# Weight sums of a fast matrix product, formed by DMA in DRAM: begun two stages earlier, each in a tensor of its own

## The chip, the cores and the metric

One core of one Trainium2 chip runs the kernel. The metric is the device time of one execution in microseconds (us). The engines that matter are TensorE (PE, matrix products), VectorE (DVE), ScalarE (ACT), GpSimd (POOL) and SyncE (SP, which issues most DMA transfers here). All of them run their own instruction lists in order and meet through semaphores.

## The reference

One encoder layer on 512 positions of width 2048, in float32:

```python
h = rms_norm(x) * (1.0 + scale[:, None]) + shift[:, None]
aq, ak, av, ag, gq, gk, gv, gg, lr_f, lr_b = jnp.split(h @ w_in[layer], PROJ_SPLITS, axis=-1)
# 16 heads of attention over three dilated windows, merged by their denominators
a_out = att.reshape(B, S, ATT_WIDTH) * jax.nn.silu(ag)
# 4 heads of gated linear attention (GLA), scanned in both directions
g_out = g_o * jax.nn.silu(gg)
y = jnp.concatenate([a_out, g_out], axis=-1) @ w_out[layer]
return rms_norm(x + gate[:, None] * y) * final_gain
```

`scale`, `shift` and `gate` come from a product of `silu(c)` with a 2048 x 6144 matrix.

## The kernel before

Every large product is made from float32 numbers split in two parts, hi and lo; three PE products (hi hi, hi lo, lo hi) take the place of one. A weight tile of 512 KB is loaded by SP (`fetch`) into one of four `raw` buffers, ACT makes its hi part, DVE its lo part (`split_hi`, `split_lo`).

The stages follow each other on PE, whose order is written by hand:

1. Stages `a` and `b`: 16 steps of k each, with the sums that give `scale` and `shift` beside them. A planner (`_plan`) with due times orders the other engines here.
2. Units `qk2`, `qk4`, `qk6`, `gk`: eight groups of weights each, with the attention of two pairs of heads mixed in. The keys' halves (`ks`, `kl`) are moved by small DMAs from POOL's queue.
3. The v stage (GLA's values) as a fast matrix product: seven block products `a b f c d e f g` in place of eight, 28 steps of 512 KB weights. Some weight operands are sums of quadrants of the weight matrix: T1 = B11+B12, T2 = T1+B22, T3 = T2+B21, U = B12+B22. Some left operands are sums of quadrants of h, kept in DRAM and loaded as 256 KB halves (`hrb` to `hre`, by `h_load`).
4. Gated units `ag0`, `ag1`, `gg0`, `gg1`, with the four GLA heads and the sums for `vbias` and `gate` (`sumv`, `sumg`: loads of 512 KB or 1 MB that DVE multiplies and adds up) mixed in.
5. The output stage: two fast matrix products (pair 0 and pair 1), with the same sums T1, T2, T3, U of `w_out`'s quadrants; at last the final norm and the stores.

The weight sums cost PE nothing: DMAs on POOL's queue form them in DRAM. `sum_begun` (L333) copies one 512 KB quarter of the first operand into the sum's tensor, `sum_ended` (L336) adds the second operand to it (an accumulating DMA). `weight_sums` issues them from the list `sum_dmas`, so many per weight group as `SUM_DMAS` says; a small POOL instruction on the group's hi part (`seen`, L351) holds them back until that group has been split. `sum_in_place` adds T2 onto T1's tensor, and T3 onto T2's, where no copy is made; it can start only when the last load of the old sum has landed, so these additions run inside the v stage (T2 beside product `b`, T3 beside `c`) and inside the output stage (T3 beside `c` of either pair).

On SP the loads stand in one list. In the v stage step z asks for the weights of step z+3 first and then for h's halves up to step z+3. The framework's scheduler orders ACT, DVE, POOL and SP outside stages `a` and `b` by priority and by when data is ready, except where `keep_in_program_order` pins them.

In the GLA scan (`states`, L874 to L900) DVE writes a state into half 0 of the tile `pair`, POOL multiplies it by the decay into half 1 (L892), and DVE adds the next product to that into half 0 again (L894); ACT scales each state for PE (L899).

Of the kernel before, what the change touches and what calls it, by code (L numbers as in the profile page):

```python
# [10 lines left out]
F32 = mybir.dt.float32  # L11
# [3 lines left out]
ALU = mybir.AluOpType  # L15
# [6 lines left out]
KT = D // P  # L22
# [111 lines left out]
def block_kernel(ctx: ExitStack, tc: tile.TileContext, a: dict):  # L134
# [200 lines left out]
    def sum_ended(pair, name, q):  # L335
        return nc.gpsimd.dma_start(dsum[pair, name, q], quadrant(pair, SUMS[name][1], q), accum_op=ALU.add,  # L336
                                   max_dma_last_dim=4096)
# [431 lines left out]
    def sum_of(kind, m):  # L769
# [15 lines left out]
        def part(z, c, to, first):  # L785
# [22 lines left out]

    def some_sums(name, how="halves", lead=1.0, begin=0.0):
        r = next_sums(SUMS_IN.get(name, len(sum_work)), how)  # L810
        if begin:
            r = [(load, lambda go=go: tc.keep_in_program_order(go())) for load, go in r]
        n = len(r) / (1 - begin)
        loads = [(max(begin + (q + 0.7 - lead) / n, 0.1 / n), x[0]) for q, x in enumerate(r)]
        return sorted(loads + [(begin + (q + 0.7) / n, x[1]) for q, x in enumerate(r)], key=lambda x: x[0])

    def gla_head(h):
# [57 lines left out]
        def states(d):  # L875
            def go():
# [7 lines left out]
                for j, c in enumerate(x["order"]):  # L884
                    o = 256 * (j % 2)
                    kv = pkv[j // 2][:, o:o + 256]
                    st = pair[:, 0, :]
                    if prev is None:
                        nc.vector.tensor_scalar(st, kv, sc[:, 2, c:c + 1], None, op0=ALU.mult)  # L889
                    else:  # L890
                        dc = pair[:, 1, :]
                        nc.gpsimd.tensor_scalar(dc, prev, sc[:, 1, c:c + 1], 1.0,  # L892
                                                op0=ALU.mult, op1=ALU.mult)
                        stt(st, kv, sc[:, 2, c:c + 1], dc, op0=ALU.mult, op1=ALU.add)  # L894
# [70 lines left out]
    def unit(name, natural, side=(), lr=None):  # L965
# [5 lines left out]
        for g in range(KT // 2):  # L971
# [505 lines left out]
    for pair, n, q in steps:  # L1477
# [152 lines left out]
```

## Time and profile before

| | |
|---|---|
| median of 3 runs | 937.34 us (937.13 to 938.41) |
| the profiled execution's own time | 938.63 us |
| its span, first to last instruction | 936.9 us |
| TensorE busy | 911.5 us, 97% of the span |
| VectorE, ScalarE, GpSimd busy | 718.1, 482.9, 144.1 us |
| DMA queue q1 (SP) | 182.11 MB, 53.8% of 16 engines' span |
| DMA queue q0 (POOL) | 51.52 MB, 23.2% of 16 engines' span |
| granted TensorE clock, mean | 0.993 |

In a row of a view by stretches stand, for each engine, its busy us and in brackets its instructions, then the granted clock, the DMA engines' mean busy share and the GB/s moved. In a row of a timeline stand start, duration, engine, line and operation; the bracket at its end says how long the engine had waited and for whom. SPq is SP's queue of DMA issues.

### The profile page before, as it was taken

How to read it: one execution, taken by the hardware profiler on the slowest of the kernel's cores; microseconds unless marked ns; L12 is line 12 of the kernel's file. 1: busy time of each engine (PE TensorE's matmuls, PEld its weight loads, DVE VectorE, ACT ScalarE, POOL GpSimd, SP SyncE). 2: the span in 40 equal slices, each digit the busy share in tenths (PEclk: the TensorE clock that was granted, in tenths of full speed). 3: DMA queues.
4: the chain of work that ended last, by engine and by line, in shares of the span. 5: the costliest groups of instructions: out<-in, count | busy, mean ns of one | idle time of the engine just before them, and what ended most of it. 6: DMA issues, size and time to landing. Idle time of an engine off the chain costs nothing.

```text
span 936.9 us, 11887 instructions
## 1 busy us (share of the span) xinstructions
PE 911.5 (97%) x4225; PEld 748.9 (80%) x4225; DVE 718.1 (77%) x1071; ACT 482.9 (52%) x771; POOL 144.1 (15%) x221
## 2 busy tenths in 40 slices
PE   9999999999999999999989999979999999999995
PEld 7888888888888888888767888868888888788785
DVE  7998899688878788898726986657696769577386
ACT  4543533564655555555525744534464448445355
POOL 7400000051332321221110022111111000000100
PEclk9999999999999999999999999999999999999998
DMA  9999796498996886896999785676554458967954
GB/s 338 412 411 416 266 314 237 136 316 226 251 328 237 223 241 183 222 252 182 326 258 300 258 291 196 221 201 202 160 180 142 172 181 296 316 216 235 308 200 180
DMA packets 60044, 234.95 MB, mean 251 GB/s; under 512 B 7784, under 2 KB 8336, under 8 KB 53584
## 3 DMA queue, kind: packets, MB, share of 16 engines
q1 hardware_dynamic: 48176, 182.11, 53.8%
q0 software_dynamic: 11376, 51.52, 23.2%
q8 instruction: 33, 0.54, 0.2%
q10 hardware_dynamic: 432, 0.55, 0.2%
q14 instruction: 27, 0.22, 0.1%
HBM read 220.44 MB, written 51.46 MB: 290 GB/s over the span
## 4 chain that ended last, share of the span: by engine, by line
PE 74%; DMA 13%; DVE 7%; issue 2%; ACT 2%; SPq 0%; DVEq 0%; ACTq 0%
PE op L1469 6%; DMA sumg<-in_wg 6%; PE ps_qk L168 5%; PE ps_qk L169 5%; PE ps_qk L170 5%; PE stb L170 3%; PE stb L168 3%; PE stb L169 3%; PE o L728 3%; PE sta L169 3%; PE vp L1149 3%; PE sta L170 3%; PE sta L168 3%; PE t L715 3%; PE oq L1469 3%; PE ps_gg L168 3%
## 5 line engine op out<-in xcount | busy, mean ns | idle before, releaser
L269 DVE CUSTOM_DVE_ANT_0 cb<-cb,sb,c_bcond 128x2048 f32<-128x2048 f32 (+1 forms) x32 | 74.0, 2313 | 6.0 <-DMA cb<-in_wm 5.9
L702 ACT ACTIVATE p<-p,st 128x512 f32<-128x512 f32 x64 | 46.0, 719 | 24.2 <-DVE st L699 22.3
L699 DVE CUSTOM_DVE_ANT_0 p<-s,g 128x512 f32<-128x512 f32 x64 | 43.4, 682 | 1.7 <-PE s L696 1.5
L336 POOL DMA_DIRECT2D T<-in_w_o x24 | 17.7, 736 | 165.3 <-DMA raw_o0c<-T 93.3
L269 DVE CUSTOM_DVE_ANT_0 sumg<-sumg,sb,c_bcond 128x1024 f32<-128x1024 f32 (+1 forms) x16 | 23.7, 1483 | 19.4 <-DMA sumg<-in_wg 19.4
L715 PEld LDWEIGHTS t<-c_ident,p 128*128 128x128 f32 x256 | 31.8, 141 | 8.4
L715 PE MATMUL t<-c_ident,p 128*128 128x128 f32 x256 | 38.3, 272 | 0.0
L704 DVE TENSOR_SCALAR p<-p,st 128x512 f32<-128x512 f32 x64 | 31.0, 485 | 1.7
L269 DVE CUSTOM_DVE_ANT_0 sumg<-sumg,sb,gate 128x1024 f32<-128x1024 f32 x13 | 16.7, 1282 | 17.3 <-DMA sumg<-in_wg 17.3
L899 ACT ACTIVATE sq<-pair,sc 128x256 f32<-128x256 f32 x24 | 12.2, 507 | 27.9 <-DVE pair L889 16.9
L695 PE MATMUL s<-ks,qs 128*128 128x512 f32 x64 | 25.3, 395 | 0.0
L696 PE MATMUL s<-kl,qs 128*128 128x512 f32 x64 | 25.0, 391 | 0.0
L1024 POOL DMA_DIRECT2D gqd<-gqt x1 | 0.6, 586 | 151.3 <-ACT gqt L537 151.3
L703 DVE RECIPROCAL st<-st 128x1 f32<-128x1 f32 x64 | 10.2, 159 | 12.6 <-ACT p L702 12.5
L291 POOL TENSOR_SCALAR lnm<-lnm,rel 16x207 f32<-16x207 f32 (+7 forms) x14 | 18.9, 1363 | 5.0 <-DMA lnm<-in_lnm 5.0
L473 ACT ACTIVATE h_hi<-xt,shift 128x512 fp32r<-128x512 f32 x16 | 11.4, 719 | 11.3 <-DVE shift L269 11.3
L731 ACT ACTIVATE pair<-o 64x512 f32<-64x512 f32 x16 | 9.5, 595 | 14.9 <-PE o L728 14.8
L336 POOL DMA_DIRECT2D T1v<-in_w_gv x12 | 9.4, 783 | 47.4 <-DMA raw_ovb<-T1v 28.9
L930 PE MATMUL go<-qi,sq 128*128 128x128 f32 x96 | 15.9, 275 | 0.0
L892 POOL TENSOR_SCALAR pair<-pair,sc 128x256 f32<-128x256 f32 x16 | 8.6, 537 | 47.2 <-DVE pair L889 41.2
L269 DVE CUSTOM_DVE_ANT_0 sumv<-sumv,shb 128x1024 f32<-128x1024 f32 (+1 forms) x8 | 11.9, 1488 | 5.0 <-DMA sumv<-in_wv 5.0
L932 ACT ACTIVATE gsq<-go 128x512 f32<-128x512 f32 x8 | 4.8, 597 | 21.1 <-PE go L930 21.1
(1841 smaller groups left out, 3244.3 us busy)
## 6 DMA issues: line engine op xcount, KB each, us to landing
cb<-in_wm SPq DMA_DIRECT2D x31, 1024.0 KB, 11.3
T<-in_w_o POOLq DMA_DIRECT2D x32, 512.0 KB, 7.9
sumg<-in_wg SPq DMA_DIRECT2D x26, 512.0 KB, 4.2
raw_qk<-in_w_qk SPq DMA_DIRECT2D x24, 512.0 KB, 5.3
rawb<-in_w_sb SPq DMA_DIRECT2D x16, 512.0 KB, 6.4
T1v<-in_w_gv POOLq DMA_DIRECT2D x16, 512.0 KB, 9.7
U<-in_w_o POOLq DMA_DIRECT2D x16, 512.0 KB, 8.1
raw_ag<-in_w_ag SPq DMA_DIRECT2D x16, 512.0 KB, 4.5
```

The costliest lines, as they stand in the source:

```text
L168: mm(ps, lh, rh, start=first, stop=False)
L169: mm(ps, ll, rh, start=False, stop=False)
L170: mm(ps, lh, rl, start=False, stop=last)
L269: return nc.vector.tensor_tensor_reduce(out=w, in0=w, in1=with_, op0=ALU.mult, op1=ALU.add, scale=1.0, scalar=init, accum_out=dst)
L336: return nc.gpsimd.dma_start(dsum[pair, name, q], quadrant(pair, SUMS[name][1], q), accum_op=ALU.add, max_dma_last_dim=4096)
L699: nc.vector.tensor_tensor_reduce(out=t, in0=ps, in1=gt[h][:, P * i:P * i + 512], op0=ALU.add, op1=ALU.min, scale=1.0, scalar=3e38, accum_o ...
L702: act(t, t, AF.Exp, bias=st[:, 0:1], scale=-1.0, accum_out=st[:, 1:2])
L704: nc.vector.tensor_scalar(t, t, st[:, 2:3], None, op0=ALU.mult)
L715: nc.tensor.transpose(pk[:, kt * P:kt * P + P], t[:, kt * P:kt * P + P], ident)
L728: mm(po, vv[h // 4][:, kt, h % 4, :], parts[w][:, kt, :], start=kt == 0 and w == 0, stop=kt == 3 and w == 1)
L1149: mm(ps, l_, r_, start=first and x == 0, stop=last and x == 2, skip_group_check=not new)
L1469: mm(ps[:, c], l_, r_[:, c], start=first and z == 0, stop=last and z == 2, skip_group_check=not new)
```

## The change

Four things.

- `sum_in_place` is gone. T2 and T3 are begun by a copy like the others and ended by an addition, so 96 transfers in place of 80: 48 additions as before, 48 copies in place of 32.
- The list starts earlier and ends later: eight copies in the second half of stage `b` (planner tasks `wsum`), 48 transfers in `qk2` to `gk` as before, four copies in the v stage, nine transfers in each gated unit (before: eight in `ag0`, eight in `ag1`, none behind them).
- In the v stage h's halves are asked for ahead of the weights. The sums `sumv` that run beside it are laid out by other positions (`sums_in_parts`).
- The GLA states alternate between the two halves of `pair`; the decayed state goes into the tile that ACT later fills with the scaled state (`sq2`).

```diff
-    def sum_in_place(pair, name, q):
-
-        dsum[pair, name, q] = dsum[pair, SUMS[name][0], q]
-        sum_ended(pair, name, q)
-
-    sum_dmas = [(f, pair, name, q) for pairs, names in ((("v",), ("T1", "U")), ((0, 1), ("T1", "U")), ((0, 1), ("T2",)))
+    sum_dmas = [(f, pair, name, q) for pairs, names in ((("v",), ("T1", "U")), (("v",), ("T2",)), (("v",), ("T3",)), ((0,), ("T1", "U")), ((0,), ("T2",)),
+                                     ((1,), ("T1", "U")), ((0,), ("T3",)), ((1,), ("T2",)), ((1,), ("T3",)))
                 for f in (sum_begun, sum_ended) for name in names for pair in pairs for q in range(4)]
...
-    SUM_DMAS = {"qk2": 2, "qk4": 2, "qk6": 1, "gk": 1, "ag0": 1, "ag1": 1, "gg0": 1}
+    SUM_DMAS = {"qk2": 2, "qk4": 2, "qk6": 1, "gk": 1, "ag0": 1.125, "ag1": 1.125, "gg0": 1.125, "gg1": 1.125}
...
+    for k in range(8, KT):
+        task(("wsum", k), "POOL", 1.5, [("wh", "b", k)] + ([("wsum", k - 1)] if k > 8 else ["rows"]), 50,
+             lambda k=k: weight_sums(spl["b", k][0], 1, lambda x: x))
...
-                    parts=[(load(2, c, b8_), part(0, c0, half, init)), (lambda: None, part(1, c1, dst, half))])
+                    parts=[(load(2, c, b8_), part(0, c0, half, init), part(1, c1, dst, half))])
...
+    def sums_in_parts(name):
+        r = next_sums(SUMS_IN[name], "parts")
+        return [((s_ // 3 + (0.02, 0.5, 0.64)[s_ % 3]) / len(r), x) for s_, x in enumerate(y for z in r for y in z)]
...
-                    st = pair[:, 0, :]
+                    st = pair[:, j % 2, :]
+                    if j % 2 == 0:
+                        sq2 = T2(f"sq{n}{j}")
...
-                        dc = pair[:, 1, :]
+                        dc = sq2[:, o:o + 256]
...
+        for y in range(z, z + 4):
+            h_load(y)
         for ahead in (2, 3):
             fetch(i + ahead)
-        if n in "bc":
-            sum_in_place("v", "T2" if n == "b" else "T3", q)
-        for y in range(z, z + 4):
-            h_load(y)
+        if z in (0, 2, 23, 25):
+            weight_sums(wts[i][0], 1)
...
-        if n == "c":
-            sum_in_place(pair, "T3", q)
```

The rows below are the instruction lists of the two kernels. In POOL's rows at the v stage, names that end in v and a digit are sums for the v stage, T202 is quarter 2 of T2 for output pair 0, `16x8192` is a copy and `128x1024` an addition. Before:

```order
L351 TENSOR_SCALAR seen_131<-gk7h_3914 1x1
L336 DMA U12_2733<-in_w_o3 128x1024
L351 TENSOR_SCALAR seen_131<-ova0h_4001 1x1
L336 DMA U13_2735<-in_w_o3 128x1024
L336 DMA T1v0_1548<-in_w_gv1 128x1024
L336 DMA T1v1_1550<-in_w_gv1 128x1024
L336 DMA T1v2_1584<-in_w_gv1 128x1024
L336 DMA T1v3_1586<-in_w_gv1 128x1024
L336 DMA T1v0_1548<-in_w_gv0 128x1024
L336 DMA T1v1_1550<-in_w_gv0 128x1024
L336 DMA T1v2_1584<-in_w_gv0 128x1024
L336 DMA T1v3_1586<-in_w_gv0 128x1024
```

And the same place now:

```order
L347 TENSOR_SCALAR seen_131<-gk7h_3934 1x1
L336 DMA T202_3602<-in_w_o1 128x1024
L347 TENSOR_SCALAR seen_131<-ova0h_4021 1x1
L336 DMA T203_3682<-in_w_o1 128x1024
L347 TENSOR_SCALAR seen_131<-ova0h_4021 1x1
L333 DMA T110_4095<-in_w_o2 16x8192
L347 TENSOR_SCALAR seen_131<-ova2h_4103 1x1
L333 DMA T111_4149<-in_w_o2 16x8192
L347 TENSOR_SCALAR seen_131<-ovf3h_4688 1x1
L333 DMA T112_4746<-in_w_o2 16x8192
L347 TENSOR_SCALAR seen_131<-ovg1h_4754 1x1
L333 DMA T113_4787<-in_w_o2 16x8192
```

The eight additions in place are gone; two copies stand at the stage's first steps (groups ova0, ova2) and two near its end (ovf3, ovg1).

POOL's rows at the start of unit `gg0`. Before:

```order
L351 TENSOR_SCALAR seen_131<-gg00h_5687 1x1
L336 DMA T213_5237<-in_w_o3 128x1024
L351 TENSOR_SCALAR seen_131<-gg01h_5751 1x1
L351 TENSOR_SCALAR seen_131<-gg02h_5814 1x1
L351 TENSOR_SCALAR seen_131<-gg03h_5884 1x1
```

And now:

```order
L347 TENSOR_SCALAR seen_131<-gg00h_5712 1x1
L336 DMA T300_5530<-in_w_o0 128x1024
L336 DMA T301_5566<-in_w_o0 128x1024
L347 TENSOR_SCALAR seen_131<-gg01h_5777 1x1
L336 DMA T302_5602<-in_w_o0 128x1024
L347 TENSOR_SCALAR seen_131<-gg02h_5841 1x1
L336 DMA T303_5665<-in_w_o0 128x1024
L347 TENSOR_SCALAR seen_131<-gg03h_5912 1x1
L333 DMA T210_5916<-T110_4095 16x8192
```

One addition at this place became four, and copies and additions go on through `gg0` and `gg1`, where before the `seen` instructions stood alone.

SP's rows in the v stage (`raw_ov` and a letter are the weights of that product, `hr` and a letter the halves of h for it, `gqb` and `sumv` other loads). Before:

```order
L359 DMA raw_ovb0_4101<-T1v0_1548 128x1024
L359 DMA raw_ovb1_4121<-T1v1_1550 128x1024
L1123 DMA hrb1_4123<-hs1_1502 128x512
L1123 DMA hrb2_4148<-hs2_1503 128x512
L779 DMA sumv52_4297<-in_wv 128x2048
L359 DMA raw_ovb2_4146<-T1v2_1584 128x1024
L359 DMA raw_ovb3_4176<-T1v3_1586 128x1024
L1113 DMA gqb_4499<-gqd_1499 128x2048
L359 DMA raw_ovf0_4203<-in_w_gv0 128x1024
L1123 DMA hrb3_4179<-hs3_1504 128x512
```

And now:

```order
L355 DMA raw_ovb0_4126<-T1v0_1133 128x1024
L1125 DMA hrb1_4144<-hs1_1526 128x512
L355 DMA raw_ovb1_4146<-T1v1_1170 128x1024
L1125 DMA hrb2_4172<-hs2_1527 128x512
L778 DMA sumv52_4481<-in_wv 128x2048
L355 DMA raw_ovb2_4174<-T1v2_1214 128x1024
L355 DMA raw_ovb3_4204<-T1v3_1256 128x1024
L1115 DMA gqb_4517<-gqd_1523 128x2048
L355 DMA raw_ovf0_4228<-in_w_gv0 128x1024
L1125 DMA hrb3_4202<-hs3_1528 128x512
```

Only `hrb1` moved here, past one weight load (further down `hrd1` and `hrd2` do the same); `hrb3` keeps its place, and the `sumv` loads keep theirs. PE's list is the same in both kernels. On ACT and DVE the split of `hpc3` moved ahead of that of the weights `ovc2`, `sq112` moved behind the four evictions of `ag0`, and DVE's two halvings of `cat0` in `ag1` moved ahead of the mask instruction on `at1`.

More of the change, by code (lines that the diff above doesn't have):

```diff
@@ L337, in sum_ended, with weight_sums @@
                                    max_dma_last_dim=4096)
-    def sum_in_place(pair, name, q):
-        dsum[pair, name, q] = dsum[pair, SUMS[name][0], q]
-        sum_ended(pair, name, q)
-    sum_dmas = [(f, pair, name, q) for pairs, names in ((("v",), ("T1", "U")), ((0, 1), ("T1", "U")), ((0, 1), ("T2",)))
+    sum_dmas = [(f, pair, name, q) for pairs, names in ((("v",), ("T1", "U")), (("v",), ("T2",)), (("v",), ("T3",)), ((0,), ("T1", "U")), ((0,), ("T2",)),
+                                     ((1,), ("T1", "U")), ((0,), ("T3",)), ((1,), ("T2",)), ((1,), ("T3",)))
                 for f in (sum_begun, sum_ended) for name in names for pair in pairs for q in range(4)]
     seen = cst.tile([1, 1], F32, tag="seen", name="seen")
-    SUM_DMAS = {"qk2": 2, "qk4": 2, "qk6": 1, "gk": 1, "ag0": 1, "ag1": 1, "gg0": 1}
-    def weight_sums(hi, most):
-        tc.keep_in_program_order(nc.gpsimd.tensor_scalar(seen, hi.bitcast(F32)[0:1, 0:1], 1.0, None, op0=ALU.mult))
+    SUM_DMAS = {"qk2": 2, "qk4": 2, "qk6": 1, "gk": 1, "ag0": 1.125, "ag1": 1.125, "gg0": 1.125, "gg1": 1.125}
+    def weight_sums(hi, most, pin=tc.keep_in_program_order):
+        pin(nc.gpsimd.tensor_scalar(seen, hi.bitcast(F32)[0:1, 0:1], 1.0, None, op0=ALU.mult))
         for _ in range(min(most, len(sum_dmas))):
             f, *which = sum_dmas.pop(0)
-            tc.keep_in_program_order(f(*which))
+            pin(f(*which))
     def fetch_o(i, pair, n, q):
@@ L807, in sums_behind_scores, with some_sums @@
         return side
-    def some_sums(name, how="halves", lead=1.0, begin=0.0):
+    def sums_in_parts(name):
+        r = next_sums(SUMS_IN[name], "parts")
+        return [((s_ // 3 + (0.02, 0.5, 0.64)[s_ % 3]) / len(r), x) for s_, x in enumerate(y for z in r for y in z)]
+    def some_sums(name, how="halves", lead=1.0):
         r = next_sums(SUMS_IN.get(name, len(sum_work)), how)
[L811 to L815, printed above, removed]
+        n = len(r)
+        loads = [(max((q + 0.7 - lead) / n, 0.1 / n), x[0]) for q, x in enumerate(r)]
+        return sorted(loads + [((q + 0.7) / n, x[1]) for q, x in enumerate(r)], key=lambda x: x[0])
     def gla_head(h):
@@ L896, in go @@
                     nx = c + 1 if d == 0 else c - 1
-                    if j % 2 == 0:
-                        sq2 = T2(f"sq{n}{j}")
                     act(sq2[:, o:o + 256], st, AF.Copy, scale=sc[:, 0, nx:nx + 1])
@@ L976, in unit @@
             if name in SUM_DMAS:
-                weight_sums(wts[todo[-1]][0], SUM_DMAS[name])
+                n = SUM_DMAS[name]
+                weight_sums(wts[todo[-1]][0], int(n * g + n) - int(n * g))
             for ahead in (1, 2):
@@ L1170, in block_kernel @@
     side += [(3 + k, lambda k=k: lr_tick(k)) for k in range(KT)] + [(18.7, low_rank), (16, gq_back)]
-    side += [(2 + 24 * at, go) for at, go in some_sums("gv", "parts", 1.7)]
+    side += [(2 + 24 * at, go) for at, go in sums_in_parts("gv")]
     heads = [x for h in range(GH) for x in gla_head(h)]
```

## The prediction

> **What bounds the kernel now.** I read the busy shares first, then PE's time by stretches, then who PE waited for.
>
> ```profile
> PE 911.5 (97%) x4225; PEld 748.9 (80%) x4225; DVE 718.1 (77%) x1071; ACT 482.9 (52%) x771; POOL 144.1 (15%) x221
> ```
>
> PE's list is the bound, and its instructions don't change. So the change is worth what it does to the places where PE stands still:
>
> ```profile
> 12.00:460.00 448.00, 447.90 (x2095) 369.07 (x2095) 379.76 (x630) 234.86 (x395) 92.73 (x137) 1.00 0.85 274
> 460.00:500.00 40.00, 34.91 (x138) 25.14 (x137) 17.74 (x21) 14.56 (x21) 4.88 (x6) 0.96 1.02 289
> 500.00:510.00 10.00, 10.00 (x45) 7.65 (x44) 7.48 (x8) 6.47 (x9) 0.00 (x0) 1.00 0.87 300
> 600.00:630.00 30.00, 24.97 (x137) 20.95 (x136) 16.15 (x24) 12.71 (x18) 5.07 (x9) 1.00 0.74 183
> 630.00:680.00 50.00, 48.85 (x246) 40.94 (x245) 35.49 (x51) 24.27 (x42) 7.72 (x15) 1.00 0.66 190
> 680.00:800.00 120.00, 119.93 (x561) 99.89 (x560) 91.52 (x119) 65.73 (x94) 7.91 (x12) 1.00 0.59 199
> 800.00:810.00 10.00, 9.12 (x39) 6.83 (x39) 3.88 (x4) 3.87 (x5) 1.62 (x2) 1.00 1.02 345
> 810.00:820.00 10.00, 10.00 (x46) 8.29 (x45) 8.26 (x10) 6.30 (x9) 0.00 (x0) 1.00 0.85 277
> 870.00:880.00 10.00, 8.11 (x29) 6.21 (x28) 3.67 (x3) 3.55 (x4) 1.61 (x2) 0.83 0.96 302
> ```
>
> PE is full to 460 us. Where only products of 512 columns run, the count of instructions tells more than the busy time: undisturbed, 10 us hold 45 or 46 of them. The v stage's 460 to 500 holds 138, which is 138/4.5 = 30.7 us of work in 40: **9.3 us** lost. In the output stage 800 to 810 holds 39 (1.5 us lost) and 870 to 880 holds 29 (3.7 us): **5.2 us**. The gated units lose 5.0 us (600 to 630) and 1.2 us (630 to 680). The waits give the names:
>
> ```profile
> PE gn L945 <- DVE gsl L943: 3.6, 2, 2.8
> PE vq L1149 <- ACT hpb3h L1129: 2.5, 1, 2.5
> PE oq L1469 <- ACT keep1b L1425: 1.9, 1, 1.9
> ```
>
> **The v stage.** The longest wait, for `hpb3h`, is a wait for data:
>
> ```profile
> 452.79 0.33 SPq L779 DMA_DIRECT2D sumv<-in_wv  x1
> 462.34 0.37 SPq L1123 DMA_DIRECT2D hrb<-hs  x1
> 475.34 0.63 ACT L1129 ACTIVATE hpb3h<-hrb 128x512 fp32r<-128x512 f32 x1 [7.73 <-DMA hrb<-hs]
> 478.94 0.81 POOL L336 DMA_DIRECT2D T1v<-in_w_gv  x1 [11.46 <-DMA raw_ovc<-T1v]
> 488.46 0.81 POOL L336 DMA_DIRECT2D T1v<-in_w_gv  x1 [5.12 <-DMA raw_ovc<-T1v]
> SPq L359 <- DMA T1v<-in_w_gv: 5.2, 1, 5.2
> 464.00:468.00 4.00, 3.54 (x15) 2.29 (x14) 3.00 (x5) 3.53 (x5) 1.61 (x2) 1.00 1.02 424
> 468.00:477.00 9.00, 6.44 (x27) 4.40 (x26) 1.61 (x3) 1.62 (x3) 0.00 (x0) 0.95 1.02 265
> 481.00:497.00 16.00, 14.45 (x60) 10.23 (x58) 5.19 (x6) 4.99 (x7) 2.47 (x3) 1.00 1.02 235
> ```
>
> A 256 KB half took 13 us. The three stretches say why: the DMA engines are full in all of them (share 1.02), but move 424 GB/s where loads run alone and 235 to 265 where additions of POOL's queue run too. From 481 to 497 they moved 16 x 0.235 = 3.76 MB, which at 424 would take 8.9 us; 7.1 us more went into the four additions issued from 478.94 to 488.46. So one **addition costs** 1.8 us beyond the 1.24 us that its own 0.524 MB take: 3.0 us of all 16 engines. A copy has no row of its own; I take the 1.24 us of its bytes as its cost, with 3.0 us, the addition's, as the upper end. In the same 16 us the loads got 3.76 - 4 x 0.524 = 1.66 MB, 104 GB/s: a 512 KB load beside additions takes 5.0 us instead of 1.24.
>
> The change takes eight additions (24 us) out of this stage and puts two copies at its start (2.5 us). At 460 us the backlog ahead of `hrb3` is then loads alone: `sumv`, two weight tiles, `gqb` and `ovf0`, 3.7 MB issued from 452.8 on, 8.7 us at 424 GB/s plus one copy, so `hrb3` lands near 465 instead of 475; PE, whose wait of 2.5 us ended with this split at 476.0, wants it at 473.5. The 5.2 us for which SP stood behind an unfinished sum go too, and with them what followed: weights `ovc2`, `ovc3` and the halves `hrc1` to `hrc3` queued behind. Ends: all 9.3 us, or, if `hrb3` alone stays late, nothing of its wait and half clock (2.5 + 1.7 us), so 5.1. I take **-8.5**, near the full end, since the stage behind (500 to 510) runs loads at 300 GB/s and loses nothing. The new order of SP's rows is worth 0: it moves `hrb1`, `hrd1` and `hrd2` by one load each (1.24 us). ACT now splits `hpc3` ahead of `ovc2`; with `hrc3` landing some 8 us ahead of need that is free, without that cover it costs one step, 12 products or 2.7 us.
>
> The clock is part of these losses: 0.96 over 40 us is 1.6 us, 0.83 over 10 us is 1.7, and both are inside the 9.3 and the 3.7. The Trainium skill (TensorE: Matmul & The Clock Gate, Part 1) says that an idle window of about 3.4 us halves the clock and that the window runs freely. The trace agrees only in part: a wait of 1.9 us was enough at 872 us, one of 2.8 us in 600 to 630 was not (clock 1.00). The rule speaks against this change: a wait of 4 us in the gated units would bring 1.7 us more, and by it the sum below would end 1.7 us higher.
>
> **The output stage.** Eight additions in place go, four beside `c` of each pair.
>
> ```profile
> 857.58 1.88 SPq L1307 DMA_DIRECT2D x<-in_x  x4
> 859.92 0.61 SPq L359 DMA_DIRECT2D raw_o1c<-T  x1
> 872.97 1.06 ACT L403 ACTIVATE o1c1h<-raw_o1c 128x1024 fp32r<-128x1024 f32 x1 [5.10 <-DMA raw_o1c<-T]
> 873.93 0.58 ACT L1425 ACTIVATE keep1b<-oq 128x512 f32<-128x512 f32 x1
> 803.80 1.06 ACT L403 ACTIVATE o0d2h<-raw_o0d 128x1024 fp32r<-128x1024 f32 x1 [3.15 <-DMA raw_o0d<-in_w_o]
> ```
>
> `raw_o1c` took 13 us behind four loads of `x` (2.1 MB) and one addition; without the addition it lands 3.0 us sooner, at 869.9, and ACT is through with it and with `keep1b` (1.06 + 0.58) by 871.6. PE, whose wait of 1.9 us ended with `keep1b` at 874.5, arrives at 872.6. So that wait and its half clock go, with 1.0 us to spare. `raw_o0d` has two additions beside it: 6 us sooner for a wait of 1.5. Ends: 5.2, or 1.5 if the 1.0 us don't hold. I take **-5.0**.
>
> **The gated units** get it back in part. DVE waits there for loads that it must add up in order, and a half's buffer comes free only after the half before it:
>
> ```profile
> DVE sumg L269 <- DMA sumg<-in_wg: 36.7, 20, 5.2
> 609.96 1.28 DVE L269 CUSTOM_DVE_ANT_0 sumg<-sumg,sb,c_bcond 128x1024 f32<-128x1024 f32 x1 [3.39 <-DMA sumg<-in_wg]
> 621.09 1.28 DVE L269 CUSTOM_DVE_ANT_0 sumg<-sumg,sb,gate 128x1024 f32<-128x1024 f32 x1 [5.16 <-DMA sumg<-in_wg]
> 669.23 1.29 DVE L269 CUSTOM_DVE_ANT_0 sumg<-sumg,sb,c_bcond 128x1024 f32<-128x1024 f32 x1 [1.57 <-DMA sumg<-in_wg]
> 677.36 1.28 DVE L269 CUSTOM_DVE_ANT_0 sumg<-sumg,sb,gate 128x1024 f32<-128x1024 f32 x1 [3.23 <-DMA sumg<-in_wg]
> 678.57 0.69 DVE L943 TENSOR_TENSOR gsl<-gsq,gsh 128x512 fp32r<-128x512 f32 x1
> 754.55 1.28 DVE L269 CUSTOM_DVE_ANT_0 sumg<-sumg,sb,gate 128x1024 f32<-128x1024 f32 x1 [3.54 <-DMA sumg<-in_wg]
> ```
>
> - `ag0`: additions stand where three copies stood, 3 x 1.8 us more; no wait shows there (500 to 600 is full), so 0, and up to 2.
> - `ag1`: at its first group two additions replace one copy, so the half used at 609.96 comes up to 3.8 us later, which the mask on `at1` and PE behind it feel at once. But the next half, at 621.09, meets additions at the same points as before, and the wait that ends the stretch (`gn`, behind it) then ends where it did. Later copies replace four additions. I take **+1**, ends -1.5 and +4.
> - `gg0`: four additions stand in a row where one stood, 9 us more, across the halves used at 669.23 and 677.36. The first comes 2.5 us later (two loads share 104 GB/s until the additions are through), the second, issued behind it, 3 us later, and `gsl` with it, for which PE already waits: **+3**. Ends 0 and 7.6 (two halves, 3.8 each).
> - `gg1`: from nothing to five additions, four copies and the three additions of `gg0`'s last groups, 29 us at most, in a stretch with DMA share 0.59. PE never waited here and the weights are split one group, 24 products or 5.3 us, ahead; the halves at 754 us are 3.5 us late already. **+1.5**, ends 0 and 4.
>
> Sum: **+5.5**, ends -1.5 and +17.6.
>
> **Costs of nothing.** The eight copies in stage `b` (10 us) lie under this row: PE is full and the DMA engines are busy for 0.58.
>
> ```profile
> 155.00:205.00 50.00, 50.00 (x226) 41.40 (x225) 37.62 (x62) 27.36 (x47) 10.78 (x21) 1.00 0.58 192
> 200.00:280.00 80.00, 80.00 (x391) 65.99 (x390) 64.09 (x136) 45.50 (x85) 25.09 (x41) 1.00 0.97 282
> DVE pair L894 <- POOL pair L892: 8.8, 14, 0.7
> T<-in_w_o POOLq DMA_DIRECT2D x32, 512.0 KB, 7.9
> ```
>
> Ends 0 and 1.2, the first keys' copy waiting behind one. `qk2` to `gk` keep 48 transfers, four copies turned into additions: 7 us more in 240, while `qk2`, at a share of 0.97, swaps four itself. Its weights need 0.52 MB per group, and a group with nothing but its 24 products, 5.3 us, gets 0.55 MB at 104 GB/s even beside additions. Queued on POOL behind a new wait (T2's copy on T1's addition, four groups, so at least 21 us after its issue) are the keys' halves for the scores; such a transfer lands after 7.9 us, so the wait has ended by then. 0, up to 3. The state buffers: DVE's additions wait for POOL in 14 of 16 steps, and that product stays in the chain; ACT's reading of the old state, which the second buffer frees, came earlier. 0, ends -1.2 and 0.
>
> **Sum.** 938.63 - 8.5 - 5.0 + 5.5 = 930.6 us for an execution like the profiled one. That one is 1.3 us above the median of the runs, so the forecast is **929.3**. Its own range is 925 to 934.
>
> **Rivals.**
>
> - *The gated units hide everything* (chance 0.20). For: DMA share 0.59 from 680 on, PE full there. Against: 36.7 us of DVE's waiting for exactly these loads. 938.63 - 13.5 - 1.3 = 923.8.
> - *The halves stay late* (0.15). For: `hrb3` keeps its place behind `gqb` and a weight tile, and an order that hardly moved can't help it. Against: 424 GB/s without additions. 929.3 + 4.2 = 933.5.
> - *The load only moved* (0.13), and the kernel is slower. The change adds 16 copies and removes no transfer; from the last group of `ag0` to the end of `gg1`, 17 additions stand where 8 stood, before halves that DVE takes in series: 9 x 3.8 = 34 us of delay. If over 40% of that (13.5 us) passes DVE's slack, PE loses more than it won; at one half, 938.63 - 13.5 + 17 - 1.3 = 940.8. The Trainium skill (DMA: Bandwidth & Descriptors, Issuing engines are not separate DMA queues) says that transfers of all queues run on the same 16 engines and interleave; the 104 GB/s beside additions agrees.
>
> The forecast keeps 0.52. A measurement of this kernel tells 0.2%, 1.9 us, from no change. Faster: 0.52 + 0.20 + 0.15, less 0.07 for their upper tails, 0.80; within 0.2%: 0.07; slower: 0.13. For 8 in 10 the range runs from 923.0 to 937.0, which leaves out most of the last rival and the extreme of the second.
>
> **What would show it.** Right: 460 to 500 with 170 products or more and 1.00 clock, `hr` loads landing in under 8 us, the stretches beside `c` of the output full; a longer wait of PE for `gsl` in `gg0`, with DVE's `sumg` waits above 36.7 us in total. Wrong: a wait for `hpb3h` that stays, a wait for `ks` in the `qk` units, or PE waits in the gated units above 20 us together.

## The result: slower by 0.9 %

The changed kernel took **945.95 us** (median of 4 runs, 944.51 to 948.54) against 937.87 us for the kernel before (4 runs, 937.13 to 938.41): a ratio of **1.009, 95% interval 1.0064 to 1.0115**. The forecast was 929.3 us, with 923 to 937 as the range. So the sign was wrong, and the time lies outside.

The page of the changed kernel, busy time by engine:

```profile
PE 911.8 (97%) x4225; PEld 751.8 (80%) x4225; DVE 719.0 (76%) x1071; ACT 483.7 (51%) x771; POOL 167.1 (18%) x257
```

PE does the same 4225 products in the same order in 943.4 us instead of 936.9. What differs is where it waits, and at which clock it runs behind the waits. Here are the waits of PE in the changed kernel, to be read against the three rows quoted before:

```profile
PE gn L946 <- DVE gsl L944: 9.3, 2, 5.3
PE go L931 <- DVE at L917: 4.0, 1, 4.0
...
PE op L1471 <- ACT o0a2h L399: 1.5, 1, 1.5
PE op L1471 <- DVE o0a2l L379: 1.3, 1, 1.3
PE vq L1151 <- DVE ovb0l L379: 1.1, 1, 1.1
```

The waits for `hpb3h` and `keep1b`, which the change was to remove, are gone. The wait for `gsl` (the lo part of a GLA head's squared output, made by DVE for the head's norm) has grown from 3.6 to 9.3 us, the one for `at` (a head's masked scores, also from DVE) from 2.3 to 4.0, and one for the output's weight `o0a2` is new. The reason stands in DVE's waits, of before and then of the changed kernel:

```profile
DVE sumg L269 <- DMA sumg<-in_wg: 36.7, 20, 5.2
```

```profile
DVE sumg L269 <- DMA sumg<-in_wg: 55.6, 23, 6.9
```

**A way to see where time goes.** Since the list of products is the same in both kernels, the start of the n-th product can be set against the start of the n-th product of before, for all 4225. The difference is how far PE is behind (+) or ahead (-) at that place. Two rows of the timeline, the same product in before and in the changed kernel:

```profile
728.76 0.39 PE L945 MATMUL gn<-gsl,ones 128*128 128x512 f32 x1
```

```profile
734.89 0.79 PE L946 MATMUL gn<-gsl,ones 128*128 128x512 f32 x1 [5.32 <-DVE gsl L944]
```

734.89 - 728.76: PE is 6.1 us behind here. The product just ahead of it was only 0.65 behind, so 5.5 us were lost at this one product. By stretches of before's clock, the changed kernel lost (+) or won (-):

| stretch of before, us | what runs | change, us |
|---|---|---|
| 0–457 | start, stage a, stage b, attention | +0.6 |
| 457–545 | v stage | -6.8 |
| 545–600 | `ag0` | 0.0 |
| 600–668 | `ag1` | +1.8 |
| 668–720 | `gg0` | +5.0 |
| 720–768 | `gg1` | +7.8 |
| 768–797 | start of the output, `o0a`, `o0b` | +3.3 |
| 797–end | rest of the output | -5.3 |
| | sum | +6.4 |

The spans differ by 943.4 - 936.9 = 6.5, so the table is complete to 0.1 us. Some stretches of the changed kernel, on its own clock (busy time and, in brackets, instructions of each engine; at the end the granted clock, the DMA share and GB/s):

```profile
457.00:500.00 43.00, 41.08 (x179) 31.76 (x178) 24.73 (x28) 22.29 (x29) 0.00 (x0) 1.00 0.77 269
665.00:680.00 15.00, 10.97 (x57) 9.09 (x56) 7.93 (x11) 3.71 (x6) 0.78 (x3) 0.94 0.68 205
711.00:724.00 13.00, 13.00 (x87) 11.56 (x86) 4.46 (x7) 5.37 (x8) 4.56 (x8) 1.00 0.95 223
730.00:740.00 10.00, 5.11 (x13) 4.06 (x14) 9.24 (x14) 2.99 (x4) 0.65 (x2) 0.66 0.47 157
775.00:793.00 18.00, 15.18 (x66) 11.69 (x66) 17.80 (x23) 12.86 (x18) 0.00 (x0) 1.00 0.86 279
```

The v stage holds 179 products in its 43 us at full clock, where before held 151. From 730 to 740 PE does 13 products, and the clock is 0.66. In before the stretch from 711 to 724 looked like this, with a DMA share of 0.41 where it is now 0.95:

```profile
711.00:724.00 13.00, 13.00 (x87) 11.77 (x86) 6.46 (x9) 5.51 (x8) 0.00 (x0) 1.00 0.41 151
```

**How the wait in `gg1` comes about** can be followed row by row. POOL's queue first, then SP's, then DVE's, all of the changed kernel:

```profile
711.37 0.48 POOL L895 TENSOR_SCALAR sq<-pair,sc 128x256 f32<-128x256 f32 x1 [1.68 <-DVE pair L897]
...
711.98 0.83 POOL L336 DMA_DIRECT2D T<-in_w_o  x1
...
712.78 1.86 POOL L336 DMA_DIRECT2D T<-in_w_o  x2
...
717.02 0.66 POOL L336 DMA_DIRECT2D T<-in_w_o  x1
```

```profile
710.84 5.12 SPq L778 DMA_DIRECT2D sumg<-in_wg  x2
...
725.34 0.33 SPq L778 DMA_DIRECT2D sumg<-in_wg  x1
```

```profile
714.31 1.28 DVE L269 CUSTOM_DVE_ANT_0 sumg<-sumg,sb,c_bcond 128x1024 f32<-128x1024 f32 x1 [1.95 <-DMA sumg<-in_wg]
...
724.01 1.28 DVE L269 CUSTOM_DVE_ANT_0 sumg<-sumg,sb,gate 128x1024 f32<-128x1024 f32 x1 [5.89 <-DMA sumg<-in_wg]
...
730.53 1.28 DVE L269 CUSTOM_DVE_ANT_0 sumg<-sumg,sb,c_bcond 128x1024 f32<-128x1024 f32 x1 [4.62 <-DMA sumg<-in_wg]
...
731.74 2.49 DVE L1018 TENSOR_TENSOR cat<-cat,sgg 128x512 f32<-128x512 f32 x4
734.15 0.68 DVE L944 TENSOR_TENSOR gsl<-gsq,gsh 128x512 fp32r<-128x512 f32 x1
```

POOL held its additions back behind the state products of the GLA scan (the weights `gg07`, for which the first of them waited, were split at 700.6) and then issued four of them in 5 us. The half loaded beside them (the second of the two at 710.84, issued at 715.63) came only at 724.0. Its buffer's next half could be asked for at 725.34 and came at 730.5. `gsl` stands on DVE behind both, so it ran at 734.15; before it ran at 727.27:

```profile
717.00 1.28 DVE L269 CUSTOM_DVE_ANT_0 sumg<-sumg,sb,gate 128x1024 f32<-128x1024 f32 x1
...
723.29 1.29 DVE L269 CUSTOM_DVE_ANT_0 sumg<-sumg,sb,c_bcond 128x1024 f32<-128x1024 f32 x1 [0.75 <-DMA sumg<-in_wg]
...
727.27 0.69 DVE L943 TENSOR_TENSOR gsl<-gsq,gsh 128x512 fp32r<-128x512 f32 x1 [0.28 <-ACT gsh L942]
```

Behind the wait for `gsl` comes a second loss. The next products of PE in the changed kernel:

```profile
735.48 0.63 PE L168 MATMUL ps_gg<-h_hi,gg10h 128*128 128x512 f32 x1
735.91 0.63 PE L169 MATMUL ps_gg<-h_hi,gg10l 128*128 128x512 f32 x1
```

They start 0.43 us apart instead of 0.23, which is half clock. A clock of 0.66 over the 10 us from 730 on is 10 x 0.34 / 0.5 = 6.8 us at half rate; the part of it that lies behind the wait cost 7.8 - 5.5 = 2.3 us. The same happens behind the waits for `gsl` in `gg0` (678.14) and for `at` in `ag1` (610.80):

```profile
610.80 0.55 PE L931 MATMUL go<-at,gv 128*128 128x128 f32 x1 [4.04 <-DVE at L917]
```

```profile
610.00:617.00 7.00, 6.20 (x30) 6.23 (x31) 3.09 (x4) 0.60 (x1) 0.00 (x0) 0.52 0.77 263
```

### The profile page after: what moved, and what is told of

It reads as the page before. It is cut to its first block, busy times and chain, and to the rows that moved or that the text cites. A ratio compares the mean times of both kernels' runs of the same rounds, so it can differ in the third digit from the quotient of the medians.

```text
span 943.4 us, 11955 instructions
## 1 busy us (share of the span) xinstructions
PE 911.8 (97%) x4225; PEld 751.8 (80%) x4225; DVE 719.0 (76%) x1071; ACT 483.7 (51%) x771; POOL 167.1 (18%) x257
## 4 chain that ended last, share of the span: by engine, by line
PE 76%; DMA 12%; DVE 6%; issue 3%; ACT 2%; SPq 1%; DVEq 0%; POOL 0%; ACTq 0%; POOLq 0%
DMA sumg<-in_wg 9%; PE op L1471 7%; PE ps_qk L168 5%; PE ps_qk L169 5%; PE ps_qk L170 5%; PE oq L1471 5%; PE vp L1151 3%; PE stb L169 3%; PE stb L168 3%; PE stb L170 3%; PE o L727 3%; PE sta L169 3%; PE sta L170 3%; PE sta L168 3%; PE t L714 3%
## 5 line engine op out<-in xcount | busy, mean ns | idle before, releaser
L931 PE MATMUL go<-at,gv 128*128 128x128 f32 x64 | 14.1, 305 | 4.0 <-DVE at L917 4.0
```

Source lines behind the costliest of these rows:

```text
L931: mm(po[:, cs], l, r, start=i == 0, stop=i == len(terms) - 1)
```

## The experiments

Two theories stood at first. *Place*: additions hurt where they hit the few groups in which DVE stands just ahead of PE. *Amount*: it is their number in the gated units that counts, wherever they stand in them. All kernels keep PE's list, so the table by stretches can be made for each, against the same execution of before. It says where (the expectations give 15.8 and 10.0 us for what the table has as 16.1 and 10.2; they cut the stretches a little differently). The median and the ratio say how much, because a stretch comes from one profiled execution, and executions of one kernel differ by several microseconds. The stretches aren't independent either: a kernel that has lost less so far reaches the next one earlier, and can wait longer there for the same load. Each ratio is taken to the executions of before that ran beside that kernel.

| kernel | median, us | ratio to before, 95% | before 457 | v | `ag0` | `ag1` | `gg0` | `gg1` | `o0a` | rest |
|---|---|---|---|---|---|---|---|---|---|---|
| changed | 945.95 | 1.009, 1.0064–1.0115 | +0.6 | -6.8 | 0.0 | +1.8 | +5.0 | +7.8 | +3.3 | -5.3 |
| b_states | 938.23 | 1.000, 0.9981–1.002 | 0.0 | +0.5 | 0.0 | -1.4 | 0.0 | 0.0 | 0.0 | -1.1 |
| b_halves | 942.61 | 1.0049, 1.0027–1.0071 | +0.5 | +5.3 | +0.9 | +1.4 | -1.0 | 0.0 | 0.0 | -3.1 |
| a_halvesback | 949.30 | 1.0129, 1.0085–1.0172 | +0.2 | -7.4 | +4.4 | +1.5 | +5.6 | +7.2 | +1.2 | -5.3 |
| a_moved | 934.90 | 0.9962, 0.9942–0.9982 | +4.4 | -7.8 | +0.2 | +2.6 | +0.2 | 0.0 | 0.0 | -5.0 |
| a_copies | 941.96 | 1.002, 0.9996–1.0044 | +0.1 | -7.5 | +0.1 | +0.8 | +3.3 | +1.7 | +5.2 | -5.3 |
| a_drop | 931.62 | 0.9941, 0.9924–0.9959 | +0.5 | -7.7 | +0.1 | +1.7 | +0.6 | 0.0 | +1.3 | -5.3 |
| a_groups | 948.34 | 1.0102, 1.0072–1.0132 | +0.7 | -7.0 | +7.6 | +3.3 | +7.1 | +0.4 | +6.8 | -5.3 |
| a_early | 926.47 | 0.9863, 0.9834–0.9893 | 0.0 | -9.3 | +5.2 | -3.6 | +0.3 | 0.0 | 0.0 | -5.3 |
| a_light | 933.62 | 0.9956, 0.9932–0.998 | +4.6 | -9.3 | +9.1 | -6.0 | -1.1 | 0.0 | 0.0 | -5.2 |
| a_even | 928.74 | 0.9882, 0.9852–0.9913 | +2.0 | -9.3 | +3.1 | -2.3 | +4.2 | 0.0 | 0.0 | -5.2 |

### The state buffers alone

The kernel before, with the change's own lines for the GLA states and nothing else:

```diff
-                    st = pair[:, 0, :]
+                    st = pair[:, j % 2, :]
+                    if j % 2 == 0:
+                        sq2 = T2(f"sq{n}{j}")
...
-                        dc = pair[:, 1, :]
+                        dc = sq2[:, o:o + 256]
```

> The kernel before with only the two state buffers of the GLA scan. By the step of the prediction it is worth between -1.2 and 0 us: 936.7 to 937.9. Rival: the product that now goes into sq2 ties POOL to ACT's turn of sq2 (ACT's first sq of a head moved behind a table load), and at costs 1 to 2 us more before go: 939 to 940.

938.23 us, ratio 1.000. The part is worth nothing that can be measured, as its step had it; the rival falls.

### The order of h's halves, alone and undone

Alone, in the kernel before:

```diff
+        for y in range(z, z + 4):
+            h_load(y)
         for ahead in (2, 3):
             fetch(i + ahead)
         if n in "bc":
             sum_in_place("v", "T2" if n == "b" else "T3", q)
-        for y in range(z, z + 4):
-            h_load(y)
```

> The kernel before with only the halves of h queued ahead of the weights in the v stage; the sums in place stay. By the step of the prediction the order is worth 0: 937.9 within 0.9 us. Rival, from the trace of the changed kernel, whose PE fell behind by 1.6 us at ovb0 and ovb1 (457 to 470 us): the halves ahead of weights make sumv and ovb0 late, and the time is 939.0 to 940.0.

942.61 us: 4.2 us slower than the 938.39 of before in the same runs, so neither of the two numbers came. PE fell back by 5 us not at `ovb0` but at `ovc2`. ACT's timeline of this kernel:

```profile
499.71 0.63 ACT L1129 ACTIVATE hpc3h<-hrc 128x512 fp32r<-128x512 f32 x1 [2.96 <-DMA hrc<-hs]
500.25 1.04 ACT L403 ACTIVATE ovc2h<-raw_ovc 128x1024 fp32r<-128x1024 f32 x1
```

`hpc3` now stands ahead of `ovc2` in ACT's row, its half was still on its way, and `ovc2` waited behind it. In the changed kernel that cover was there: `hpc3h` ran at 484.34 with 0.82 us of waiting. The other way round, the changed kernel with `h_load` behind `fetch` and the weight sums again:

```diff
-        for y in range(z, z + 4):
-            h_load(y)
         for ahead in (2, 3):
             fetch(i + ahead)
         if z in (0, 2, 23, 25):
             weight_sums(wts[i][0], 1)
+        for y in range(z, z + 4):
+            h_load(y)
```

> The changed kernel with one part undone: in the v stage the halves of h are queued behind the weights again; the spread sums stay. Alone in the kernel before, that part cost 4.2 us, because the split of hpc3 stood ahead of ovc2 on ACT and DVE while hrc3 was still on its way (PE 5 us late at ovc2). Theory 1: without additions in place hrc3 lands in time (in the changed kernel hpc3 was split at 484.3, well ahead of its products), so only the 1.6 us lost at ovb0 and ovb1 (sumv behind the halves) come back: 944.3 us, between 943 and 946. Rival: the halves ahead are what saves the 6.8 us of the v stage, and undoing them costs up to 6: 948 to 952.

949.30 us, 3.4 above the changed kernel where theory 1 had it 1.6 below; the intervals (1.0085 to 1.0172 and 1.0064 to 1.0115) overlap. By the time alone the rival would have won. But the stretches say otherwise: the v stage came out at -7.4 instead of -6.8, 0.6 us better, so the order of the halves isn't what won it. (The other positions of the `sumv` loads, which this kernel keeps, were not tried alone.) The profiled execution (946.08) lost 4.4 us in `ag0`, which the edit doesn't touch: PE waited 2.6 us there for `pair`, and the clock halved behind it. The changed kernel queued the same transfers there and had no such wait. Why is open.

### Transfers moved from the last units into the attention units

```diff
-    SUM_DMAS = {..., "qk6": 1, "gk": 1, "ag0": 1.125, "ag1": 1.125, "gg0": 1.125, "gg1": 1.125}
+    SUM_DMAS = {..., "qk6": 2, "gk": 2, "ag0": 1.5, "ag1": 1}
```

> The changed kernel with one table altered: two transfers a group also in qk6 and gk, 1.5 a group in ag0, one a group in ag1, none in gg0 and gg1; the same 96 transfers, all of the computation. Theory 1 (place): PE lost 4.8 us in gg0, 8.0 in gg1 and 3.0 at o0a2 because additions stand there before loads that DVE takes in series; under the products of qk6 and gk, whose rows show PE full, they cost nothing. Then 945.9 - 15.8 = 930 us, between 927 and 934. Rival (the load only moves): the transfers' time on the 16 DMA engines comes up again wherever they stand, qk6 to ag0 lose what gg0 and gg1 win, and the time stays within 942 to 948.

934.90 us, just above the theory's range and far below the rival's. `gg0`, `gg1` and `o0a` lose 0.2 us instead of 16.1. Theory 1 had that right, but 4.4 us came back earlier: 1.1 us at `kl` (POOL's queue) and 3.1 at `ova2`. Four additions, issued from 434.6 to 437, stand there ahead of a half of the v stage's sum; the changed kernel issues two, and has that half at 452.35 instead of 457.29:

```profile
457.29 1.23 DVE L269 CUSTOM_DVE_ANT_0 sumv<-sumv,shb 128x1024 f32<-128x1024 f32 x1 [4.52 <-DMA sumv<-in_wv]
...
459.77 1.22 DVE L379 TENSOR_TENSOR ova2l<-raw_ova,ova2h 128x1024 fp32r<-128x1024 f32 x1
```

So it is the same thing at another place: a sum on DVE, a load that shares the engines with additions, and a weight behind the sum.

### The last twelve additions: as copies, and left out

```diff
+    COPIED = [(0, "T3", q) for q in range(4)] + [(1, n, q) for n in ("T2", "T3") for q in range(4)]
...
-            pin(f(*which))
+            if f is sum_ended and tuple(which) in COPIED:
+                pin(nc.gpsimd.dma_start(dsum[tuple(which)], quadrant(which[0], SUMS[which[1]][1], which[2])))
+            else:
+                pin(f(*which))
```

> The changed kernel with its last twelve additions (0 T3, 1 T2, 1 T3, issued in gg0, gg1 and beside o0a) replaced by plain copies of the same 512 KB; the additions themselves are left out, so T2 of pair 1 and T3 of both pairs hold no sums. Issue points, bytes and order stay. Theory 1 (an addition holds the 16 engines 3.0 us, a copy 1.24): twelve times 1.8 us of backlog goes, PE's loss in gg0, gg1 and at o0a2 falls from 15.8 to 6.5 us (in the ratio 1.24 to 3.0), and the time is about 936.6 us, between 933 and 940. Rival (any transfer of this size at these points delays the loads behind it as much, since it is their number in front of a half and not their kind that counts): within 943 to 948.

The second kernel issues nothing for these twelve. In both, the sums concerned are left incomplete: they tell time only.

```diff
-            pin(f(*which))
+            if not (f is sum_ended and tuple(which) in LEFT_OUT):
+                pin(f(*which))
```

> The changed kernel with its last twelve additions (0 T3, 1 T2, 1 T3) left out and nothing in their place, so that T2 of pair 1 and T3 of both pairs hold copies and no sums; the copies stay where they are. Against the run in which plain copies stand in the additions' place (loss of PE in gg0, gg1 and at o0a 10.0 us instead of the 15.8 of the changed kernel). Theory 1, as amended (what counts is the time on the DMA engines of all that stands before DVE's loads, additions 3.0 us, copies some 1.3): without the twelve the loss is below 3 us, and the time 931 to 935. Rival (the copies of T2 and T3 that stay in gg0 and gg1 delay the loads by themselves): 6 us or more stay, 936 to 940.

Left out: 931.62 us, and 1.9 us remain in the three stretches. As copies: 941.96 us, and 10.2 us remain (its profiled execution took 936.94, 5 us below its median, so that is rather too little). The 941.96 lies between the theory's range (933 to 940) and the rival's (943 to 948), so it confirms neither. The rival of the second run falls: the copies that stay in `gg0` and `gg1` cost little. In the profiles one addition there costs PE (16.1 - 1.9)/12 = 1.2 us and a copy (10.2 - 1.9)/12 = 0.7. By these two the ratio of 1.24 to 3.0 that I had taken is too favourable to copies, but that isn't shown stage by stage: `o0a` lost more with copies (+5.2 instead of +3.3), and PE also reached it 10 us earlier there. (The prediction said that a copy had no row of its own. The DMA view of before has one: eight copies `T<-T`, which landed after 4.8 us in the median.)

### The same number at other groups

```diff
-    SUM_DMAS = {... "ag0": 1.125, "ag1": 1.125, "gg0": 1.125, "gg1": 1.125}
+    SUM_DMAS = {... "ag0": [2, 2, 2, 2, 2, 2, 1, 0], "ag1": [0, 0, 1, 2, 2, 2, 1, 0],
+                "gg0": [0, 0, 1, 2, 2, 2, 1, 0], "gg1": [0, 0, 1, 2, 2, 2, 0, 0]}
```

A list gives the number of transfers for each of a unit's eight groups.

> The changed kernel with the same 36 transfers in the four gated units, in the same order, at other groups: ag0 2,2,2,2,2,2,1,0 a group, ag1 0,0,1,2,2,2,1,0, gg0 0,0,1,2,2,2,1,0, gg1 0,0,1,2,2,2,0,0. No addition is issued from the last group of a unit to the second group of the next, where the GLA head's DVE chain stands, nor beside o0a. Theory 1 (place): PE's losses at gsl in gg0 and gg1 and at o0a2 (15.8 us together) were due to additions in just those groups; at least three quarters go: 930 to 934 us. Rival (amount): the 36 transfers cost the DMA engines the same time, DVE's sums arrive as late and PE waits at other tiles of the same units: 940 us or more.

948.34 us: *place* falls. No wait for `gsl` is left among PE's, but others took its place:

```profile
PE kv L884 <- DVE pair L898: 9.0, 2, 5.6
PE kt L872 <- DVE ki L862: 5.5, 1, 5.5
PE go L932 <- DVE at L918: 1.8, 2, 1.2
```

`pair` and `ki` stand on DVE behind sums just as `gsl` does, and DVE's waits for the halves come to 53.5 us here. `gg1` itself loses only 0.4 us here, but `o0a` behind it 6.8 instead of 3.3, though no addition is issued beside it. So these other groups are no better; that no group at all would be free was not tried.

### Sums begun earlier

```diff
-    SUM_DMAS = {"qk2": 2, "qk4": 2, "qk6": 1, "gk": 1, "ag0": 1.125, "ag1": 1.125, "gg0": 1.125, "gg1": 1.125}
+    SUM_DMAS = {"qk2": [2] * 8, "qk4": [2] * 8, "qk6": [2] * 8, "gk": [1] * 8, "ag0": [2] * 8,
+                "ag1": [0, 0, 1, 1, 1, 1, 1, 1]}
...
-    for k in range(8, KT):
+    for k in range(KT):
...
-        if z in (0, 2, 23, 25):
+        if z in (23, 25):
```

> The changed kernel with sums begun earlier: one transfer a group in all 16 groups of stage b, two a group in qk2, qk4, qk6, one in gk, none in the first half of the v stage, two at its end, two a group in ag0, six from the third group of ag1 on, none in gg0 and gg1. Theory 1 (place): the 15.8 us of gg0, gg1 and o0a2 go, and the 4.2 us that the table of the run before lost at kl and ova2 (too many transfers in gk and at the start of the v stage) don't come: 945.9 - 15.8 - 1.5 = 928.6 us, between 926 and 932. Rival (stage b has no room: its weights come late beside copies): PE loses 3 us or more between 100 and 200 us, and the time is 932 to 936.

**926.47 us**, 925.72 to 927.10, ratio **0.9863** (0.9834 to 0.9893): faster than both kernels, and inside the range that was expected. The rival falls: stage b has room for all 16. Here is PE in its stretch, DMA share 0.93, in this kernel:

```profile
100.00:200.00 100.00, 100.00 (x445) 82.84 (x444) 87.75 (x110) 45.76 (x71) 29.15 (x44) 1.00 0.93 314
```

The v stage wins 9.3 us, against 6.8 in the changed kernel: with no copies at its start the wait at `ovb0` is gone too. (The two versions below have none there either, and win the same 9.3.) Two more versions were to take out the 5.2 us of `ag0`. The first empties `ag1` and puts five transfers in two groups of `qk4` and `qk6` (against the kernel just shown):

```diff
-    SUM_DMAS = {"qk2": [2] * 8, "qk4": [2] * 8, "qk6": [2] * 8, "gk": [1] * 8, "ag0": [2] * 8,
-                "ag1": [0, 0, 1, 1, 1, 1, 1, 1]}
+    SUM_DMAS = {"qk2": [2] * 8, "qk4": [3, 2] * 4, "qk6": [3, 2] * 4, "gk": [2, 2, 2, 2, 2, 0, 0, 0],
+                "ag0": [2, 2, 2, 2, 2, 1, 1, 0]}
```

> As the version with sums begun earlier (926.5 us), but with ag1 free too and fewer in ag0: one a group in stage b, two in qk2, 3 and 2 by turns in qk4 and qk6, two in the first five groups of gk, two at the end of the v stage, twelve in ag0; all of the computation. Theory 1, as amended (every transfer in the gated units costs PE, those in the attention units none while they stay ahead of the v stage): the 1.9 us that PE still lost against before in ag0 and ag1 go, 923 to 926.5. Rival (qk4 and qk6 have no room for five in two groups: the keys' halves come late on POOL's queue): PE waits of 2 us or more for kl or ks, 927 to 931.

The second has one a group in `ag0`:

```diff
+    SUM_DMAS = {"qk2": [2] * 8, "qk4": [3, 2] * 4, "qk6": [2] * 8, "gk": [2, 1, 1, 1, 1, 1, 1, 1],
+                "ag0": [1] * 8, "ag1": [0, 0, 1, 1, 1, 1, 2, 2], "gg0": [0, 0, 1, 0, 0, 0, 0, 0]}
```

> As the version with sums begun earlier (926.5 us), with ag0 back to one transfer a group instead of two: four more in qk4, one more in gk, two more in ag1 and one in gg0 take the rest; all of the computation. Where ag0 had two a group PE lost 5.2 us at the keys' values of its second head (kv behind the state buffers, 597 us of the kernel before), and 7.6 and 9.0 us in two other versions; at 1.125 a group 0.1 to 3. Theory (rate: one transfer a group fits beside a unit's weights and sums, two don't): ag0 loses under 1 us, and the time is 922 to 926. Rival (the loss is only shifted: before loses 5.0 us at 600 to 630 in the same units anyway, and a late ag0 makes that wait shorter): 926 to 929.

933.62 and 928.74 us: neither is better. In a_light PE lost 4.6 us before the v stage: 1.7 at `t` in `qk6`, behind a load (`g`) that DVE waited for, and 2.3 at `ks` and `kl`, which is its rival's mechanism. `ag0` lost 9.1. The time is above both ranges. In a_even `ag0` still lost 3.1 where under 1 was expected, and `gg0` lost 4.2 behind additions in the last groups of `ag1`; the time fell in the range of the rival, to which that second loss doesn't belong. So a limit of one transfer a group isn't enough. Nor does the number alone decide in `ag0`: nothing was lost there in the changed kernel with nine transfers, and 0.2 us in a_moved with twelve, where a_light lost 9.1 with twelve. Why stays open. What is lost there is partly given back in `ag1` (-2.3 to -6.0), where before has its own wait.

## Why the prediction was wrong, step by step

- **v stage: mechanism right, -8.5 predicted, -6.8 measured.** The wait for `hpb3h` went, the clock stayed at 1.00, and `hrb3` took under 5 us from issue (465.45) to split (470.36) instead of 13. 460 to 500 holds 166 products; I had named 170. The missing part is a new wait of 1.1 us at `ovb0` and what follows it, 1.6 us together. The step put the two copies at the start of the stage at "one copy" of delay to `hrb3` and left out `sumv`, which DVE takes ahead of `ovb0`. In the changed kernel:

```profile
462.62 1.23 DVE L269 CUSTOM_DVE_ANT_0 sumv<-sumv,shb 128x1024 f32<-128x1024 f32 x1 [4.12 <-DMA sumv<-in_wv]
...
463.77 1.22 DVE L379 TENSOR_TENSOR ovb0l<-raw_ovb,ovb0h 128x1024 fp32r<-128x1024 f32 x1
```

In the three kernels without these copies the stage won 9.3 us, the upper end of that term. "The new order of SP's rows is worth 0" held; "without that cover it costs one step, 2.7 us" had the mechanism and was too small: 5 us in b_halves, since ACT, DVE and the clock all follow.
- **Output beside `c`: right.** -5.0 predicted, -5.3 measured, at the two products that were named, and between -5.0 and -5.3 in every kernel without the additions in place.
- **Costs of nothing: right for stage b (0.0), the attention units (0.0) and the state buffers (ratio 1.000).** The +0.6 before 457 arises in the first 20 us, where executions of all kernels scatter by as much. The cover in stage b was as large as stated, and larger: it took twice as many.
- **`ag0` and `ag1`: right in number, in `ag1` partly by luck.** 0 and +1 predicted, 0.0 and +1.8 measured. The wait for `at` came later, as predicted (+1.8). The half clock behind it, 2.8 us, was not in the term, and the wait of 2.75 us for `gsl` that before had here was gone, since PE now arrived after it.
- **`gg0`: too small.** +3 predicted, +5.0 measured, inside its ends. The wait grew from 0.86 to 4.03 us, as predicted (+3.2). What the term lacked was the half clock behind it, the rest of the 5.0, some 1.7 us.
- **`gg1`: the step that failed.** +1.5 predicted with an end of +4, +7.8 measured: 5.5 us at `gsl` and 2.3 us of half clock behind it. The step named as cover "the weights are split one group ahead" and the DMA share of 0.59. Neither covered it. The first product that DVE could delay was not a weight's but `gsl`, which in `gg0` the prediction had itself found behind a half. In `gg1` it stands in the same place, only with 0.8 us to spare (in before `gsl` ended at 727.96 and its product started at 728.76), and the prediction didn't go to that row. The share of before said nothing about the 13 us from 711 to 724 either: it was 0.41 there, below the average, and the change itself filled them to 0.95, because POOL let four additions go within 5 us.
- **The start of the output: a term that was missing, +3.3.** The last four additions were counted in `gg1`, but POOL issued them from 757.5 to 769, beside the last halves of the sums and the weights of `o0a`. DVE's gating of `cat` stands behind these sums, ACT's split `s571h` behind `cat`, and `o0a2h` behind that:

```profile
774.90 1.28 DVE L269 CUSTOM_DVE_ANT_0 sumg<-sumg,sb,gate 128x1024 f32<-128x1024 f32 x1 [2.55 <-DMA sumg<-in_wg]
...
778.39 1.89 DVE L1018 TENSOR_TENSOR cat<-cat,sgg 128x512 f32<-128x512 f32 x3
...
782.11 1.06 ACT L1227 ACTIVATE s571h<-cat 128x1024 fp32r<-128x1024 f32 x1 [2.88 <-DVE cat L1244]
783.08 1.04 ACT L399 ACTIVATE o0a2h<-raw_o0a 128x1024 fp32r<-128x1024 f32 x1
```

In before the last of these sums ran at 761.58, 13 us earlier, while PE was only 8.4 us earlier when it came to this stage.

With the measured terms the sum is -6.8 - 5.3 + 14.6 + 3.3 + 0.6 = +6.4, where -8.0 was forecast (-8.5 - 5.0 + 5.5). Of the 14.4 us of error, 6.3 are `gg1`, 3.3 `o0a`, 2.0 `gg0`, 1.7 the v stage, and 1.1 the small ones.

**The rivals.** "The load only moved" is what happened, by its own mechanism, with the half clock on top. It set the point where it decides at 40% of 34 us in the gated units, and 14.6 us, 43%, were lost there, the half clock behind the waits included, which the rival doesn't have. Its price of 940.8 us was too low because `o0a` was not in it and it took the full gains. It had 0.13; the row of 36.7 us of DVE's waiting, which I quoted against the opposite rival, would have borne much more. "The gated units hide everything" and "the halves stay late" fell.

**The clock.** The prediction set aside the rule of the Trainium skill (TensorE: Matmul & The Clock Gate, Part 1), that an idle window of about 3.4 us halves the clock, because a wait of 1.9 us had been enough and one of 2.8 us had left the clock at 1.00; it named 1.7 us as what a wait of 4 us would add by it. The changed kernel's trace agrees with the rule: behind the waits of 4.04 us in `ag1` (0.52 from 610 to 617) and of 4.03 us in `gg0` (0.94 from 665 to 680) the clock falls, and the 6.8 us at half rate around the wait of 5.32 us are two of its windows. As a lower limit the 3.4 us don't hold here: waits of 2.14 us in a_early and 2.57 us in a_halvesback halved the clock too, one of 2.56 us in a_copies didn't. The three dips of the changed kernel cost 2.8 + 1.7 + 2.3 = 6.8 us after the waits had ended, more than the 6.4 us by which it fell behind. By this count the change would have won about nothing without them, where -8.0 was forecast: the half clock made it slower, but somewhat more than half of the error lies in the waits.

**What was named as showing it.** The longer wait for `gsl` in `gg0` and sums above 36.7 us (55.6) came, as written. "PE waits in the gated units above 20 us together" was to be the sign of a wrong forecast and didn't come (9.3 + 4.0 + 0.7 us): a threshold in named waits misses the half clock behind them and the output stage.

## What to carry to other kernels

A transfer that "fits" by the DMA share of the kernel before can still decide the time if it stands ahead of loads that an in-order engine takes in series: list, for each stretch that gets new traffic, every product of PE that depends on that engine, and its slack in the trace. Price the new traffic in the burst in which its queue will let it go, not at its mean rate, and follow the queue past the end of the stage. Work that must be done some time belongs under the stage whose consumers don't wait for the same queue: a transfer cost PE nothing in stage b and `qk2`, and an addition about 1.2 us in the last gated units.

## What the runs showed of the hardware that I had not expected

- Wherever PE waited 3.4 us or more for one product, from 20 us after the start on, the clock halved behind the wait: 3.45 in a_even, 4.03, 4.04 and 5.32 in the changed kernel, 3.74, 4.64 and 4.71 in a_halvesback, 4.10 in a_moved, 4.13 in a_copies and in a_drop, 5.54 and 5.62 in a_groups. In the changed kernel this cost 1.7 to 2.8 us on top. Some shorter waits halved it too.
- Plain copies of 512 KB in place of accumulating ones saved 4 us by the medians (6.6 by the ratios), where their time on the engines had suggested 9. Leaving the twelve out saved 14.
- The executions of one kernel differ by unlike amounts: 925.72 to 927.10 us (4 runs) for a_early, 946.06 to 958.08 (6 runs) for a_halvesback, 933.99 to 943.42 (35 runs) for before. That the waits for loads of two queues make the difference was not tried.
